# Hymba decoder layer: where split weights are rounded, where sample rows are summed, and when weights are made ready

## The chip, the cores and the metric

The kernel runs on one core of a Trainium2 chip. The core has a matrix engine (TensorE, PE in the profile), three engines for elementwise work (VectorE or DVE, ScalarE or ACT, GpSimd or POOL), and SyncE (SP), whose queue here issues nearly all transfers between the chip's memory (HBM) and the core's SBUF. PE writes its sums into PSUM, which has eight banks of 128 partitions by 512 fp32 numbers. The metric is the device time of one execution in microseconds, as the median of some runs.

## The reference

One layer for a prompt of 2048 rows and for a sample group of 32 rows (8 × 4), with the same weights, all in fp32. `_project` is an RMSNorm and a matrix of 1024 by 2560, `_swiglu` is (silu(h·w_gate) * (h·w_up))·w_down of the normed rows h:

```python
    q, k, v, u, vg = _project(x, norm1_g, w_in)
...
    gate = _spatial_gate(vn, sgu_w, sgu_b).reshape(B, S, D_SGU)
    x = x + jnp.concatenate([att, u * gate], axis=-1) @ w_out
    x = x + _swiglu(x, norm2_g, w_gate, w_up, w_down)
```

Attention has eight heads with three dilated windows each. The hidden width of the FFN is D_FF = 2816, which is 22 units of 128. Results are the rows of both groups after a last RMSNorm, the keys and values, and the normalised rows of the gating unit for the sample.

## The kernel before

**Precision.** PE multiplies a rounded fp32 format. Each fp32 operand is split into a high part (a copy that rounds, made on ACT) and a low part (the rest, a subtraction on DVE or POOL), and each product is three matmuls: high·high, high·low, low·high. So each weight tile costs one ACT copy and one subtraction before PE can use it, in place: the low overwrites the loaded tile.

**Stages.** By the trace: 0–545 us projection, to 850 attention, to 990 the out-projection of the first block, then the FFN of three blocks of rows. Block 0 has 6 tiles of 128 rows (about 990–1455), block 1 has 6 (1560–2030), the last block 4 tiles and the 32 sample rows (2140–2506). Between blocks lies a transition (`next_block`), in which the last down products of the one block are mixed with the out-projection and norms of the next.

**FFN.** Hidden units are taken in pairs. For each unit, seven products (Strassen's scheme over two halves of the columns and of the rows) are made by `one(u, q)`, one per tick of a clock; `later(n, fn)` puts a piece of work n ticks ahead, so the order of all engines is that in which Python emits the pieces. A pair n has seven down products `k = 7n + p`, each at a tick `t_ = 14(n + 1) + SLOT[p]`. The weight of a down product is loaded three products ahead into a ring of three places (two in `hop` tiles, one in `dwx`) and split by `split_dw`, three ticks before its product. ACT makes the high (L1651), and the low (L1652) is on DVE in block 0, on POOL in block 1, and in the last block on DVE for each third product and on POOL for the others. The seven operands of a pair's down products, made from the hidden activations, are also split (L1693, L1689). POOL's main work is the low of the streamed gate and up weights (`op`, L1589), on which it spends 518.8 us. PE's down matmuls are L1667, and DVE adds each result to the rows kept in SBUF (`acc`, L1669). The up products are L1786 to L1788; their sums in PSUM (`ps_m`) are taken out by DVE into `raw` and `zn` (L1798 to L1815).

**Sample rows of the last block.** `hs4` holds the sample's hidden values as 64 columns a unit: high and low side by side, so a product with 64 stationary columns (L1676) gives both parts in the two halves of the partitions. In four of seven down products the sample's rows are multiplied too, into a fresh bank, and DVE adds the bank to the 64-row accumulator once or twice (L1680).

**Transitions.** The output weights are kept as eight pairs of high and low tiles; `half1_place` puts four of them in places that hop tiles leave ("woh", "wol"), `half1_split` splits them (ACT L137, POOL L140) at ticks 14, 16, 18, 20, and `sources` loads the next block's weights for the up products at 16, 18, 20, 22. `split_cat` splits the concatenated attention rows on DVE and POOL in turn. SP's queue holds these loads, the stores of finished rows (`out_yp`) and the loads of the next rows (`acc`) in one order.

**Weight sums.** Strassen's scheme needs sums of down weights. `down_rows` loads them, `down_sums` adds on POOL (tile `tw`, L629), `down_keep` stores them; a plan places them at steps of the projection, pair n from step 124 + 9n. A step is about 2.3 us.

Of the kernel before, what the change touches and what calls it, by code (L numbers as in the profile page):

```python
# [10 lines left out]
F32 = mybir.dt.float32  # L11
# [8 lines left out]
P = 128  # L20
# [44 lines left out]
def hymba_step(ctx: ExitStack, tc: tile.TileContext, A: dict, O: dict):  # L65
# [1269 lines left out]
    def load_acc(B, i):  # L1335
# [4 lines left out]
        else:  # L1340
            dve.memset(x[SR:2 * SR], 0.0)
# [307 lines left out]
    def split_dw(B, k):  # L1649
        hi, lo_ = B.dw[k]  # L1650
        act.activation(hi, lo_.bitcast(F32), AF.Copy)  # L1651
        (dve if B.b0 == 0 or B.last and k % 3 == 0 else pool).tensor_sub(lo_, lo_.bitcast(F32), hi.bitcast(F32))  # L1652

    def down_product(B, k):
# [15 lines left out]
        if B.last and p in (0, 4, 5, 6):  # L1670
            if p < 6:
                B.chain["s"] = ps_m(3)
            ps = B.chain["s"][0:2 * SR]
            hs_ = hs4[:, n % 2 * 2 + (p in (4, 6))]
            for y, r_ in enumerate((dh, dl)):
                pe.matmul(ps, hs_, r_, start=(p < 6 and y == 0), stop=(y == 1), skip_group_check=True)  # L1676
            x = B.acc[B.nt]
            for half in ((0, 1), (0,), (), (1,))[(0, 4, 5, 6).index(p)]:
                cs = slice(half * 512, (half + 1) * 512)
                dve.tensor_add(x[0:2 * SR, cs], x[0:2 * SR, cs], ps)  # L1680
# [59 lines left out]
    def h_last(B, u, part):  # L1740
# [19 lines left out]
        else:  # L1760
# [4 lines left out]
            lows_of(B, 5, u["s1"], 0, n)  # L1765
            lows_of(B, 6, u["s4"], 0, n)
# [62 lines left out]
    def hidden(B, u, zz, c):  # L1829
# [9 lines left out]
        if B.last:  # L1839
            hs_ = hs4[:, f // 2 % 2 * 2 + f % 2]  # L1840
            hi, lo_ = (hs_[:, v * SR:(v + 1) * SR].rearrange("p (z j o c) -> p z j o c", z=2, o=2, j=B.nt // 2)[:, zz] for v in range(2))
# [3 lines left out]
            else:  # L1845
                dve.tensor_sub(lo_, h[:, :, :, 64:], hi.bitcast(F32))

    def plain_down(B, i, half, z, ps, start, stop):

        nr = P if B.rows[i] == P else 2 * SR  # L1850
        dh, dl = B.dw["plain", z, half]
        if nr == P:
            hh, hl = (x[:, i // 2 * P:(i // 2 + 1) * P] for x in B.hop[(0, 2, 4, 3)[2 * z + i % 2]])
            pairs = ((hh, dh), (hh, dl), (hl, dh))
        else:
            hs_ = hs4[:, (NF // 2 - 1) % 2 * 2 + z]
# [560 lines left out]
```

## Time and profile before

| | us |
|---|---|
| median of three runs | 2540.61 (2535.99 to 2541.87) |
| profiled execution | 2534.4 |
| its span, first to last instruction | 2532.6 |
| PE busy | 2410.7 (95%) |
| DVE, POOL, ACT busy | 1705.0, 1457.5, 1236.6 |
| lows of down weights, `hop`, on POOL, DVE | 92.4 (71), 87.0 (72) |
| mean granted clock of PE | 0.984 |

The profiled execution is faster than the median of the timed runs; a sum made from its rows is made against its own time. An engine's busy share is a mean over stages; the waits are read by stage. In a timeline row the number in brackets is how long the engine stood idle before the instruction, and behind the arrow is what released it. L1652 is a line of the kernel before; lines of the changed kernel are a few to twenty higher behind the first edits.

### The profile page before, as it was taken

Reading aid. Unit: us, or ns where it says so; the run is one execution under the profiler, and the core shown is the slowest. Engines: PE = TensorE matmul, PEld = TensorE weight load, DVE = VectorE, ACT = ScalarE, POOL = GpSimd, SP = SyncE. Lnnn points to the kernel's source line nnn. Section 1 sums busy time; section 2 is a strip of 40 time slices with the busy share of each in tenths; the row PEclk is TensorE's granted clock in tenths of the full one; section 3 lists DMA queues with packets and bytes.
Section 4 is the critical chain, followed back from the end, with each engine's and each line's share of the span. In section 5 each row is a group of like instructions: output and inputs, shape, how many; then the busy total and the mean of one; then the engine's idle time right before and its main releaser. Section 6 shows DMA issues by size and latency. Waiting matters only on the chain.

```text
span 2532.6 us, 40744 instructions
## 1 busy us (share of the span) xinstructions
PE 2410.7 (95%) x13764; PEld 2075.1 (82%) x13764; DVE 1705.0 (67%) x3289; ACT 1236.6 (49%) x2773; POOL 1457.5 (58%) x1165
## 2 busy tenths in 40 slices
PE   9998999999999999999999999999999988999997
PEld 7876776657888678899898978999999967888886
DVE  4558673215777644777777786777777776888887
ACT  6324343226676656555566446433334345545444
POOL 2216573214777637676776734666665643767775
PEclk9999999999999999999999999999999998999999
DMA  9874877895555465777776653655555544766673
GB/s 293 272 233 145 275 240 243 268 301 195 195 187 170 118 205 165 225 223 240 237 217 216 201 170 113 198 167 182 172 181 173 161 127 143 236 221 224 213 229 118
DMA packets 331476, 512.38 MB, mean 202 GB/s; under 512 B 33063, under 2 KB 165336, under 8 KB 326148
## 3 DMA queue, kind: packets, MB, share of 16 engines
q1 hardware_dynamic: 324420, 497.72, 61.9%
q10 hardware_dynamic: 6848, 12.06, 1.7%
q8 instruction: 109, 1.79, 0.3%
q14 instruction: 99, 0.81, 0.1%
HBM read 410.42 MB, written 178.03 MB: 232 GB/s over the span
## 4 chain that ended last, share of the span: by engine, by line
PE 54%; DVE 14%; DMA 9%; ACT 8%; issue 7%; POOL 7%; SPq 1%; ACTq 0%; DVEq 0%; POOLq 0%
PE ps_o L1667 7%; PE ps_m L1786 7%; PE ps_m L1788 6%; PE ps_m L1787 6%; PE ps_m L1667 2%; PE ps_s L891 2%; PE ps_o L946 2%; PE ps_s L320 2%; DVE hop L1689 2%; PE ps_s L321 2%; ACT fr L1557 2%; PE ps_s L322 2%; ACT op L1585 2%; DVE acc L1669 2%; POOL op L1589 2%
## 5 line engine op out<-in xcount | busy, mean ns | idle before, releaser
L1589 POOL TENSOR_TENSOR op<-fr,op 128x512 fp32r<-128x512 f32 x385 | 518.8, 1362 | 194.2 <-ACT op L1585 147.0
L1786 PE MATMUL ps_m<-xh,op 128*128 128x384 f32 (+3 forms) x1904 | 608.5, 320 | 17.3 <-DVE raw L1807 11.1
L1788 PE MATMUL ps_m<-xh,op 128*128 128x384 f32 (+3 forms) x1904 | 606.1, 318 | 0.0
L1787 PE MATMUL ps_m<-xl,op 128*128 128x384 f32 (+3 forms) x1904 | 605.3, 318 | 0.1
L1786 PEld LDWEIGHTS ps_m<-xh,op 128*128 128x128 f32 x1904 | 360.7, 189 | 34.6 <-issue 15.4
L1787 PEld LDWEIGHTS ps_m<-xl,op 128*128 128x128 f32 x1904 | 360.7, 189 | 9.3 <-DVE xl L1502 0.4
L1788 PEld LDWEIGHTS ps_m<-xh,op 128*128 128x128 f32 x1904 | 360.4, 189 | 0.0
L1667 PE MATMUL ps_o<-hop 128*128 128x512 f32 x1142 | 325.0, 396 | 18.0 <-DVE acc L1669 17.1
L1669 DVE TENSOR_TENSOR acc<-acc,ps_o 128x512 f32<-128x512 f32 x448 | 290.2, 679 | 17.5 <-PE ps_o L1667 14.5
L1667 PEld LDWEIGHTS ps_o<-hop 128*128 128x128 f32 x1142 | 209.5, 188 | 59.6 <-ACT ps_t L1826 13.9
L1585 ACT ACTIVATE op<-fr 128x512 fp32r<-128x512 f32 x396 | 238.5, 619 | 0.0
L1826 ACT ACTIVATE ps_t<-zn 128x384 f32<-128x384 f32 (+1 forms) x126 | 58.3, 463 | 341.2 <-DVE zn L1809 185.1
L320 PE MATMUL ps_s<-wh,xh 128*128 128x512 f32 x480 | 199.9, 416 | 7.4 <-ACT xh L137 5.9
L321 PE MATMUL ps_s<-wl,xh 128*128 128x512 f32 x480 | 191.4, 399 | 2.0 <-DVE wl L228 2.0
L322 PE MATMUL ps_s<-wh,xl 128*128 128x512 f32 x480 | 191.3, 398 | 0.0
L1652 POOL TENSOR_TENSOR hop<-hop 128x512 fp32r<-128x512 f32 x71 | 92.4, 1302 | 106.1 <-ACT hop L1651 80.7
L1652 DVE TENSOR_TENSOR hop<-hop 128x512 fp32r<-128x512 f32 x72 | 87.0, 1208 | 88.2 <-ACT hop L1651 88.1
L538 POOL TENSOR_TENSOR pr<-kv,qb 96x512 f32<-96x512 f32 x32 | 46.0, 1439 | 168.4 <-DMA kv<-in_cache_k_dram 83.1
L320 PEld LDWEIGHTS ps_s<-wh,xh 128*128 128x128 f32 x480 | 92.6, 193 | 51.1 <-issue 23.9
L1589 POOL TENSOR_TENSOR op<-pair,op 128x512 fp32r<-128x512 f32 x63 | 82.3, 1307 | 75.9 <-ACT op L1585 72.2
L629 POOL TENSOR_TENSOR tw<-tw 128x512 f32<-128x512 f32 x44 | 60.3, 1370 | 113.3 <-DMA tw<-in_w_down_dram 86.8
L1667 PE MATMUL ps_m<-hop 128*128 128x512 f32 x384 | 119.4, 392 | 0.0
(532 smaller groups left out, 5350.7 us busy)
## 6 DMA issues: line engine op xcount, KB each, us to landing
fr<-ab_d SPq DMA_DIRECT2D x308, 256.0 KB
hop<-dd_d SPq DMA_DIRECT2D x143, 256.0 KB
out_ks_dram<-in_cache_k_dram SPq DMA_DIRECT2D x56, 512.0 KB
out_vs_dram<-in_cache_v_dram SPq DMA_DIRECT2D x56, 512.0 KB
ab_d<-fr SPq DMA_DIRECT2D x88, 256.0 KB
dwx<-dd_d SPq DMA_DIRECT2D x71, 256.0 KB
qk_d<-pair SPq DMA_DIRECT2D x64, 256.0 KB
ab_d<-pair SPq DMA_DIRECT2D x63, 256.0 KB
```

Source lines behind the costliest of these rows:

```text
L320: pe.matmul(o[j], xh[:, k, :], wh, start=(k == 0), stop=False)
L321: pe.matmul(o[j], xh[:, k, :], wl, start=False, stop=False)
L322: pe.matmul(o[j], xl[:, k, :], wh, start=False, stop=(k == KD - 1))
L629: pool.tensor_sub(x, y, z)
L1585: act.activation(ops[f, j][0], ab[f][j], AF.Copy)
L1589: (pool if f or j in POOL_LOW else dve).tensor_sub(lo_, ab[f][j], hi.bitcast(F32))
L1652: (dve if B.b0 == 0 or B.last and k % 3 == 0 else pool).tensor_sub(lo_, lo_.bitcast(F32), hi.bitcast(F32))
L1667: pe.matmul(ps, l_, r_, start=(new and y == 0), stop=(y == 2), skip_group_check=True)
L1669: dve.tensor_add(x[:, cs], x[:, cs], ps)
L1786: pe.matmul(out, wh[:, ks], xh[:, :, k], start=(k == 0), stop=False)
L1787: pe.matmul(out, wh[:, ks], xl[:, :, k], start=False, stop=False)
L1788: pe.matmul(out, wl[:, ks], xh[:, :, k], start=False, stop=(k == 3))
```

## The change

Four parts.

1. *Sample rows.* `hs4` goes. Each unit has a place of 192 columns at the end of a big tile, with zeros, 64 columns of data, and zeros or a copy of the data (`rows_at`). A window of 128 of them is the stationary operand, so the data falls into the partitions 0–63 or 64–127 or both: the half of the output columns that a product belongs to is chosen by the window, and all sample products of the block sum up in one bank of PSUM. DVE's adds per pair go; at the end two adds and three copies take the bank out (`last_rows`).
2. *Lows of down weights.* `split_dw` becomes `dw_high`, at three ticks before the product as now, and `dw_low`, at two. In the last block all lows are on POOL; block 0 keeps its own on DVE, but for the last pair.
3. *Transitions.* Output weights take their places in the order wide, wide, ob, ob, and are split at ticks 8, 10, 13, 14; their sources come at 10, 12, 15, 16; `split_cat` is on POOL throughout; the lows of operands 5 and 6 of the last pair move to POOL; the splits of the last seven down weights stand further back.
4. *Weight sums.* Pair n starts at step 118 + 7n, and its parts follow one another two steps closer.

```diff
-        s0 = 124 + 9 * n
+        s0 = 118 + 7 * n
...
-            at(s0 + 9 + part, "out", down_sums, n, part)
-        at(s0 + 13, "store", down_keep, n, 0, 1)
-        at(s0 + 14, "store", down_keep, n, 3, 2)
+            at(s0 + 7 + part, "out", down_sums, n, part)
+        at(s0 + 11, "store", down_keep, n, 0, 1)
+        at(s0 + 12, "store", down_keep, n, 3, 2)
...
-            half1[s // 2] = wide_pair("woh") if s % 4 == 0 else ob_pair("wol")
+            half1[s // 2] = wide_pair("woh") if s < 4 else ob_pair("wol")
...
-    def split_dw(B, k):
+    def dw_high(B, k):
         hi, lo_ = B.dw[k]
         act.activation(hi, lo_.bitcast(F32), AF.Copy)
-        (dve if B.b0 == 0 or B.last and k % 3 == 0 else pool).tensor_sub(lo_, lo_.bitcast(F32), hi.bitcast(F32))
+
+    def dw_low(B, k):
+        hi, lo_ = B.dw[k]
+        (pool if B.b0 or k >= 7 * (NF // 2 - 1) else dve).tensor_sub(lo_, lo_.bitcast(F32), hi.bitcast(F32))
...
         if B.last and p in (0, 4, 5, 6):
-            if p < 6:
-                B.chain["s"] = ps_m(3)
-            ps = B.chain["s"][0:2 * SR]
-            hs_ = hs4[:, n % 2 * 2 + (p in (4, 6))]
-            for y, r_ in enumerate((dh, dl)):
-                pe.matmul(ps, hs_, r_, start=(p < 6 and y == 0), stop=(y == 1), skip_group_check=True)
-            x = B.acc[B.nt]
-            for half in ((0, 1), (0,), (), (1,))[(0, 4, 5, 6).index(p)]:
-                cs = slice(half * 512, (half + 1) * 512)
-                dve.tensor_add(x[0:2 * SR, cs], x[0:2 * SR, cs], ps)
+            v = (64, 64, 0, 0)[(0, 4, 5, 6).index(p)]
+            sample_product(B, 2 * n + (p in (4, 6)), v, dh, dl, k == 0)
+
+    def rows_at(f):
+
+        i = (2 + f % 2 if f // 2 % 2 else f % 2) if f + 2 < NF else 4 + f % 2
+        return pool_["X"][0][:, 7616 + 192 * i:7808 + 192 * i]
...
+    def sample_product(B, f, v, dh, dl, start=False, stop=False):
+
+        if start:
+            B.chain["s"] = ps_m(3)
+        l_ = rows_at(f)[:, v:v + P]
+        for y, r_ in enumerate((dh, dl)):
+            pe.matmul(B.chain["s"], l_, r_, start=start and y == 0, stop=y == 1, skip_group_check=True)
...
-            lows_of(B, 5, u["s1"], 0, n)
-            lows_of(B, 6, u["s4"], 0, n)
+            lows_of(B, 5, u["s1"], 0, n, None, pool)
+            lows_of(B, 6, u["s4"], 0, n, None, pool)
...
-                later((0, 1, 5, 8, 10, 12)[j], split_cat, B, i, dve if j % 2 else pool)
+                later((0, 1, 5, 8, 10, 12)[j], split_cat, B, i, pool)
...
-            later(14 + 2 * y, half1_split, B, 2 * y, 2 * y + 1)
-            later(16 + 2 * y, sources, B, 0, *((2 * y, 2 * y + 1) if y < 3 else (6,)))
+            later((8, 10, 13, 14)[y], half1_split, B, 2 * y, 2 * y + 1)
+            later((10, 12, 15, 16)[y], sources, B, 0, *((2 * y, 2 * y + 1) if y < 3 else (6,)))
...
-        split_dw(prev, K + 1)
         h_last(prev, prev.u, 0)
         downs(K)
         h_last(prev, prev.u, 1)
+        split_dw(prev, K + 1)
+        opens(0)
         split_dw(prev, K + 2)
-        opens(0)
         h_last(prev, prev.u, 2)
         split_dw(prev, K + 3)
+        opens(1)
         split_dw(prev, K + 4)
-        opens(1)
+        downs(K + 1, K + 2, K + 3)
         split_dw(prev, K + 5)
-        downs(K + 1, K + 2, K + 3)
...
                     if x == t_ - 3:
-                        split_dw(B, k)
+                        dw_high(B, k)
+                    if x == t_ - 2:
+                        dw_low(B, k)
```

The order on three engines, before and after. On DVE in a pair of block 0, around the adds into `raw` (L1806, L1807 before; L1820, L1821 in the change). Before:

```order
L1652 TENSOR_TENSOR dwx<-dwx,hop 128x512
L1689 TENSOR_TENSOR hop<-ps_t_10730,hop 128x3x64
...
L1800 TENSOR_TENSOR zn<-zn,ps_m_10955 128x384
L1669 TENSOR_TENSOR acc_9295<-acc_9295,ps_o_10978 128x512
L1669 TENSOR_TENSOR acc_9549<-acc_9549,ps_o_10983 128x512
L1669 TENSOR_TENSOR acc_9643<-acc_9643,ps_m_10988 128x512
L1803 TENSOR_TENSOR zn<-raw,ps_m_10996 128x384
L1652 TENSOR_TENSOR hop<-hop 128x512
L1806 TENSOR_TENSOR raw<-raw,ps_m_11025 128x384
L1807 TENSOR_TENSOR raw<-raw,ps_m_10996 128x384
```

and in the change:

```order
L1814 TENSOR_TENSOR zn<-zn,ps_m_10954 128x384
L1675 TENSOR_TENSOR acc_9295<-acc_9295,ps_o_10977 128x512
L1675 TENSOR_TENSOR acc_9549<-acc_9549,ps_o_10982 128x512
L1675 TENSOR_TENSOR acc_9643<-acc_9643,ps_m_10987 128x512
L1654 TENSOR_TENSOR dwx<-dwx,hop 128x512
L1817 TENSOR_TENSOR zn<-raw,ps_m_10996 128x384
L1820 TENSOR_TENSOR raw<-raw,ps_m_11024 128x384
L1821 TENSOR_TENSOR raw<-raw,ps_m_10996 128x384
L1675 TENSOR_TENSOR acc_9295<-acc_9295,ps_o_10977 128x512
L1675 TENSOR_TENSOR acc_9549<-acc_9549,ps_o_10982 128x512
L1675 TENSOR_TENSOR acc_9643<-acc_9643,ps_m_10987 128x512
L1654 TENSOR_TENSOR hop<-hop 128x512
```

Each low (L1652, now L1654) has moved from ahead of a product's adds to right behind them. On POOL in the last block, where `op` is a streamed weight and `hop` and `dwx` the lows of down weights, before:

```order
L1652 TENSOR_TENSOR hop<-hop 128x512
L1589 TENSOR_TENSOR op<-fr,op 128x512 x2
L1652 TENSOR_TENSOR dwx<-dwx,hop 128x512
L1589 TENSOR_TENSOR op<-fr,op 128x512 x4
L1652 TENSOR_TENSOR hop<-hop 128x512
```

and in the change:

```order
L1654 TENSOR_TENSOR hop<-hop 128x512
L1588 TENSOR_TENSOR op<-fr,op 128x512 x2
L1654 TENSOR_TENSOR hop<-hop 128x512
L1588 TENSOR_TENSOR op<-fr,op 128x512 x2
L1654 TENSOR_TENSOR dwx<-dwx,hop 128x512
```

The third that was on DVE now divides the four `op` lows that stood together. On ACT in the second transition, where "woh" and "wol" are output weights and L1891 (now L1907) sums the squares of finished rows, before:

```order
L1651 ACTIVATE xh_9285<-xl_9286 128x512
L1891 ACTIVATE pair,h_9272<-acc_15602 128x1024
L137 ACTIVATE woh<-fr 128x512 x2
L1891 ACTIVATE pair,h_9272<-acc_15633 128x1024
L1435 ACT_TABLE_LOAD
L1435 ACTIVATE h_9272<-h_9272 128x1
L1891 ACTIVATE pair,h_9272<-acc_15493 128x1024
L137 ACTIVATE wol<-fr 128x512 x2
```

and in the change:

```order
L137 ACTIVATE woh<-fr 128x512 x2
L1650 ACTIVATE xh_9285<-xl_9286 128x512 x2
L137 ACTIVATE woh<-fr 128x512 x2
L137 ACTIVATE wol<-fr 128x512 x2
L1907 ACTIVATE pair,h_9272<-acc_15602 128x1024
L137 ACTIVATE wol<-fr 128x512 x2
L1907 ACTIVATE pair,h_9272<-acc_15633 128x1024
L1434 ACT_TABLE_LOAD
```

The splits of the output weights stand ahead of the first sum of squares or right behind it, instead of between the sums. On SP's queue there, two loads of `fr<-ab_d` that stood between stores of finished rows have moved ahead of the first of these stores.

More of the change, by code (lines that the diff above doesn't have):

```diff
@@ L1340, in load_acc @@
         else:
-            dve.memset(x[SR:2 * SR], 0.0)
             sync.dma_start(x[0:SR], A["x_sample"])
@@ L1839, in hidden @@
         if B.last:
-            hs_ = hs4[:, f // 2 % 2 * 2 + f % 2]
-            hi, lo_ = (hs_[:, v * SR:(v + 1) * SR].rearrange("p (z j o c) -> p z j o c", z=2, o=2, j=B.nt // 2)[:, zz] for v in range(2))
+            hs_ = rows_at(f)
+            hi, lo_ = (hs_[:, 64 + v * SR:64 + (v + 1) * SR].rearrange("p (z j o c) -> p z j o c", z=2, o=2, j=B.nt // 2)[:, zz] for v in range(2))
             act.activation(hi, h[:, :, :, 64:], AF.Copy)
@@ L1846, in hidden, with down_sample @@
                 dve.tensor_sub(lo_, h[:, :, :, 64:], hi.bitcast(F32))
+            if f % 2 == 0 and f + 2 < NF and zz == 0:
+                later(2, lambda: act.activation(hs_[:, 128:192], hs_[:, 64:128].bitcast(F32), AF.Copy))
     def plain_down(B, i, half, z, ps, start, stop):
-        nr = P if B.rows[i] == P else 2 * SR
         dh, dl = B.dw["plain", z, half]
[L1852 to L1856, printed above, removed]
-            pairs = ((hs_, dh), (hs_, dl))
-        for y, (l_, r_) in enumerate(pairs):
-            pe.matmul(ps[0:nr], l_, r_, start=start and y == 0, stop=stop and y == len(pairs) - 1)
+        hh, hl = (x[:, i // 2 * P:(i // 2 + 1) * P] for x in B.hop[(0, 2, 4, 3)[2 * z + i % 2]])
+        pairs = ((hh, dh), (hh, dl), (hl, dh))
+        for y, (l_, r_) in enumerate(pairs):
+            pe.matmul(ps, l_, r_, start=start and y == 0, stop=stop and y == len(pairs) - 1)
+    def down_sample(B):
+        tick()
+        for z in range(2):
+            for half in range(2):
+                sample_product(B, NF - 2 + z, 0 if half else 64, *B.dw["plain", z, half])
     def down_unit(B, i):
         tick()
-        nr = P if B.rows[i] == P else 2 * SR
         for half in range(2):
@@ L1868, in down_unit @@
                 plain_down(B, i, half, z, ps, z == 0, z == 1)
-            dve.tensor_add(B.acc[i][0:nr, cs], B.acc[i][0:nr, cs], ps[0:nr])
+            dve.tensor_add(B.acc[i][:, cs], B.acc[i][:, cs], ps)
     def first_downs(B, i0, i1):
@@ L1949, in last_rows @@
         act.activation(r[:, 0:2], a[:, 2:4], AF.Sqrt)
-        down_unit(B, s)
+        down_sample(B)
         newton(r[:, 0:2], a[:, 2:4])
-        y = square_tile()
-        act.activation(y[0:SR], x[s][SR:2 * SR], AF.Copy)
+        ps, y, w_ = B.chain["s"], square_tile(), square_tile()
+        for z in range(2):
+            cs = slice(z * 512, (z + 1) * 512)
+            act.activation(y[0:SR, cs], ps[64 * z + SR:64 * z + 2 * SR], AF.Copy)
+            if z:
+                act.activation(w_[0:SR, cs], ps[64:64 + SR], AF.Copy)
+            dve.tensor_add(x[s][0:SR, cs], x[s][0:SR, cs], w_[0:SR, cs] if z else ps[0:SR])
         scaled_rows(0, r[:, 0:1])
@@ L2220, in hymba_step @@
         if B.last:
-            hs4 = consts.tile([P, 4, 2 * SR], F32R, name="hs4", tag="cats")
+            sample_rows_free(B)
         nb = None if B.last else blocks[bi + 1]
@@ L2288, in one @@
                     if x == t_ - 3:
-                        split_dw(B, k)
+                        dw_high(B, k)
+                    if x == t_ - 2:
+                        dw_low(B, k)
                     if x == t_:
```

3 lines of the change are left out of this document (added).

## The prediction

> **What bounds the kernel now.** I read the page first, then the clock, then the busy time of each engine by stage, then what TensorE (PE) waited for in each stage.
>
> ```profile
> span 2532.6 us, 40744 instructions
> PE 2410.7 (95%) x13764; PEld 2075.1 (82%) x13764; DVE 1705.0 (67%) x3289; ACT 1236.6 (49%) x2773; POOL 1457.5 (58%) x1165
> ```
>
> PE is busy for 95% of the span. PE's instructions are the same in number and order before and after, so the change can win only the 2532.6 − 2410.7 = 122 us in which PE stands, and what a slow clock costs. The next view is busy time and clock in three stretches: FFN of block 0, of block 1, of the last block (columns: PE, PEld, DVE, ACT, POOL busy, granted clock, DMA share, GB/s).
>
> ```profile
> 1050.00:1450.00 400.00, 390.08 (x2035) 361.24 (x2034) 308.12 (x513) 228.09 (x577) 287.35 (x220) 1.00 0.71 222
> 1600.00:2000.00 400.00, 400.00 (x2109) 375.02 (x2108) 301.18 (x492) 158.17 (x330) 252.47 (x193) 1.00 0.56 175
> 2140.00:2500.00 360.00, 345.93 (x2275) 315.26 (x2274) 298.36 (x584) 175.44 (x417) 256.86 (x193) 1.00 0.68 220
> ```
>
> Block 1 stands for nothing: there the moved lows can only lose. Block 0 stands for 9.9 us in 400, the last block for 14.1 in 360. The waits name the releasers: first 1000–1460, then 2135–2533.
>
> ```profile
> PE ps_m L1786 <- DVE raw L1807: 11.1, 9, 1.3
> ...
> PE ps_o L1667 <- DVE acc L1669: 13.4, 15, 1.8
> ```
>
> Both FFN losses are VectorE (DVE) adds that come late, and each is caused by what stands ahead of the add in DVE's queue. The rest of PE's idle time that the change touches is in the two transitions.
>
> **Block 0: the low moves behind the next adds.** One pair of units (45.55 us) of ten, on DVE, ACT and PE:
>
> ```profile
> 1196.37 1.36 DVE L1652 TENSOR_TENSOR dwx<-dwx,hop 128x512 fp32r<-128x512 f32 x1 [1.39 <-ACT hop L1651]
> 1199.58 1.27 DVE L1669 TENSOR_TENSOR acc<-acc,ps_o 128x512 f32<-128x512 f32 x2
> 1204.16 0.69 DVE L1652 TENSOR_TENSOR hop<-hop 128x512 fp32r<-128x512 f32 x1 [2.24 <-ACT hop L1651]
> ...
> 1201.17 2.44 ACT L1557 ACTIVATE fr<-fr,g2c 128x128 f32<-128x128 f32 x8
> 1203.51 0.61 ACT L1651 ACTIVATE hop<-hop 128x512 fp32r<-128x512 f32 x1
> ...
> 1195.38 0.85 PE L1667 MATMUL ps_m<-hop 128*128 128x512 f32 x3
> 1200.71 0.39 PE L1667 MATMUL ps_o<-dwx,hop 128*128 128x512 f32 x1
> 1206.05 0.41 PE L1786 MATMUL ps_m<-xh,op 128*128 128x384 f32 x1 [1.24 <-DVE raw L1807]
> ```
>
> ACT makes the high at 1203.51 behind eight small ops (2.44 us). DVE's low waits 2.24 us for it, and the two adds into "raw" queue behind that low, so PE waits 1.24 us for a free bank. In the change this low stands three L1669 adds further back, so the "raw" adds no longer queue behind it. Gain: up to 1.24 per pair, in all the 11.1 us of the nine waits.
>
> What is late next: the dwx low ahead of it, now at 1196.37, also moves behind the L1669 adds. These are now two at 1199.58 and a third of the same kind, and end at 1199.58 + 3 × 0.64 = 1201.5. PE had finished their product at 1195.38 + 0.85 = 1196.2, so only DVE's queue holds them, and with the low gone from ahead they end up to 1.36 earlier, at 1200.1. The low then ends between 1200.8 (if it takes 0.69) and 1201.5 (1.36), and PE reads it at 1200.71: a new wait of 0.1 to 0.8 per pair. Chosen, the middle: 10 × (1.24 − 0.45) = **−8**. Bounds: −11 (no new wait), and +9 if the adds don't move up at all and the low is long (1201.5 + 1.36 − 1200.7 = 2.1 per pair), which PE's early end speaks against.
>
> The two lows of this fence, of one shape, took 1.36 and 0.69 us. The Trainium skill ("SBUF — State Buffer", section "Who interferes with whom") says that a DVE instruction with two SBUF inputs and a GpSimd instruction that reads SBUF lock each other out for a whole instruction; the trace fits, since POOL worked beside the first. By that rule a dwx low in block 0 takes the long value, the new wait is 0.8 each, and this term is −4 instead of −8.
>
> **The last block: fewer instructions on DVE, more on POOL.** Groups of 2160–2480, one of the waits, and POOL ahead of a product:
>
> ```profile
> L1652 DVE TENSOR_TENSOR hop<-hop 128x512 fp32r<-128x512 f32 x22 | 27.7, 1257 | 24.0 <-ACT hop L1651 23.9
> L1680 DVE TENSOR_TENSOR acc<-acc,ps_m 64x512 f32<-64x512 f32 x36 | 23.5, 671 | 0.0
> L1652 POOL TENSOR_TENSOR hop<-hop 128x512 fp32r<-128x512 f32 x22 | 28.9, 1313 | 27.4 <-ACT hop L1651 22.2 <-PE ps_o L1667 5.1
> L1676 PE MATMUL ps_m<-hop,hs 128*64 128x512 f32 x62 | 20.1, 390 | 0.0
> L1667 PE MATMUL ps_o<-hop 128*128 128x512 f32 x342 | 97.2, 396 | 11.4 <-DVE acc L1669 11.2
> ...
> 2375.70 0.93 PE L1667 MATMUL ps_o<-hop 128*128 128x512 f32 x3 [1.82 <-DVE acc L1669]
> ...
> 2376.07 1.27 DVE L1680 TENSOR_TENSOR acc<-acc,ps_m 64x512 f32<-64x512 f32 x2
> ...
> 2342.91 2.55 POOL L1589 TENSOR_TENSOR op<-fr,op 128x512 fp32r<-128x512 f32 x2
> 2346.22 1.30 POOL L1652 TENSOR_TENSOR dwx<-dwx,hop 128x512 fp32r<-128x512 f32 x1 [0.75 <-PE ps_o L1667]
> ...
> 2349.49 0.40 PE L1667 MATMUL ps_o<-dwx,hop 128*128 128x512 f32 x1
> ```
>
> DVE loses 27.7 us of lows and 23.5 of sample adds: 51.2 of the 298.4 us it worked in 2140–2500. The waits fall where DVE's adds trail; most are under 1.3, one low or two sample adds long. So most of 13.4 goes. The sample products get a stationary of 128 instead of 64 rows; 390 against 396 ns says that this costs about 62 × 6 ns = 0.4 us. The ten extra ACT copies stand on an engine with 185 idle us. POOL gains 22 lows of 1.313, 28.9 us, and goes from 257 to 286 of 360. That leaves 74 us idle, but a product needs its low at a moment. At 2346.22 the low ends at 2347.52, and PE reads it at 2349.49: 1.97 us to spare. In the change it starts later by one unit, behind two operand lows (2.55 us) at the worst, which makes it 0.6 late; behind one (1.28), it has 0.7 to spare. Chosen: five of 63 products late by 0.6, 3 us, and DVE's waits down to 0.4: −13.4 + 3 + 0.4 = **−10**. Bounds: −13 and +4 (28 products late by 0.6, 17 − 13).
>
> **Block 1** changes only the moment of the low, on POOL: 0 (0 to +2), hidden as long as POOL's idle 147 us (400 − 252.5) lie ahead of the products.
>
> **Transitions.** In the second one PE waits for splits of output weights:
>
> ```profile
> 2080.68 0.45 PE L1419 MATMUL ps_o<-woh,cats 128*64 128x512 f32 x1 [1.39 <-POOL woh L140]
> 2086.39 0.69 PE L1418 MATMUL ps_o<-wol,cats 128*64 128x512 f32 x1 [3.79 <-ACT wol L137]
> 2088.74 0.69 PE L1419 MATMUL ps_o<-wol,cats 128*64 128x512 f32 x1 [1.66 <-POOL wol L140]
> 2104.29 1.05 PE L1479 MATMUL ps_m<-ident,xns 32*128 32x32 f32 x8 [5.85 <-ACT xns L1466]
> ...
> 2066.44 1.06 ACT L1891 ACTIVATE pair<-acc 128x1024 f32<-128x1024 f32 x1 [18.00 <-DVE acc L1669]
> ...
> 2080.65 10.06 SPq L1544 DMA_DIRECT2D fr<-ab_d  x4
> 2091.28 0.38 SPq L1339 DMA_DIRECT2D acc<-in_x_prompt_dram  x1
> ...
> 2097.43 0.69 DVE L1424 TENSOR_TENSOR acc<-acc,ps_m 128x512 f32<-128x512 f32 x1 [4.28 <-DMA acc<-in_x_prompt_dram]
> ```
>
> ACT stands idle for 18 us ahead of 2066.44, and the splits queue behind it. In the change they come first, so the first three waits (6.8 us, with smaller ones 8.4) go. But PE then only comes earlier to the wait for "xns", and that chain hangs on a row load: issued at 2091.28, behind four loads that stood 10.06 us in SP's queue, added on DVE at 2097.43, with PE's start at 2104.29, 13.0 us after the issue. Two of those loads now stand ahead of the first store, and the two that are left still wait for operand lows behind DVE adds of units that PE now ends earlier. Half of the queue's stand gone (5 us), less a place that comes free a little later, I take 3.9 us: the load goes out at 2087.4, an estimate, and PE restarts 13.0 later, at 2100.4: **−4**. PE stands from 2104.29 − 5.85 − 8.4 = 2090.0 on, so this pause grows to 10.4. Bounds: 0 (the load gates as now) and −8.4 (the chain keeps up). In the first block's out-projection the same places are split, and PE waits for none of them now: 0.
>
> The granted clock is 0.57 in 2080–2090 after such pauses:
>
> ```profile
> 2080.00:2090.00 10.00, 3.17 (x6) 0.84 (x6) 7.98 (x16) 3.91 (x9) 5.44 (x4) 0.57 0.37 110
> ```
>
> The Trainium skill ("TensorE: Matmul & The Clock Gate", "What's actually happening") says that an idle window of about 3.4 us halves the clock until as long a busy one has passed. By it the change has one cold start where there are two now, worth an estimated 1.7 us more; the sum leaves it out.
>
> In the first transition:
>
> ```profile
> 1461.15 1.63 PE L1667 MATMUL ps_o<-hop 128*128 128x512 f32 x6 [1.01 <-DVE acc L1669]
> 1469.67 0.50 PE L1414 MATMUL ps_m<-op,xh 128*128 128x512 f32 x1 [0.84 <-POOL op L140]
> 1479.63 0.47 PE L1667 MATMUL ps_o<-xh,hop 128*128 128x512 f32 x1 [1.73 <-DVE acc L1669]
> 1494.07 0.47 PE L1667 MATMUL ps_o<-xh,hop 128*128 128x512 f32 x1 [0.57 <-DVE acc L1669]
> ```
>
> They are 4.15 us, and DVE's splits that held up its adds go to POOL: **−4**; bounds −6 (two more small waits of this kind) and +2 (POOL late by two lows, 2 × 1.3, less one of the four).
>
> **Weight sums** come earlier, into a stretch in which the DMA engines are full, and end ahead of the loads of cached values that PE waits for later:
>
> ```profile
> 300.00:320.00 20.00, 20.00 (x85) 16.34 (x85) 14.02 (x19) 4.65 (x6) 19.12 (x11) 0.92 0.96 281
> PE ps_t L599 <- DMA pr<-in_cache_v_dram: 6.2, 4, 3.4
> ```
>
> More loads at a share of 0.96 delay weights that PE needs; fewer at the end may save the late three of the four waits, 6.2 − 3.4 = 2.8. Chosen **+1**; bounds −3 and +6 (the 6.2 us of such waits a second time); PE's full 20.00 in this window says that weights have some lead. The tail's ACT copies and the one DVE memset: 0 (−1.5 to +1), since the memset stands in the pause before "xns".
>
> **Sum:** −8 − 10 + 0 − 4 − 4 + 1 = −25. The profiled execution took 2534.4 us (span 2532.6), 6.2 less than the median 2540.6; from its own time that is 2509.4, and against the median **2516**.
>
> **The rivals.**
>
> 1. *The row load gates all of the second transition, and the sums crowd the loads.* 0 instead of −4, and +6 instead of +1: 2516 + 4 + 5 = 2525. For it: the 10.06 us that SP stands, and the share 0.96. Against it: two loads of the four do move, and PE was busy for all of that window.
> 2. *DVE's waits only change place.* Each wait was a queue one instruction too long; if ACT's late highs are the true limit (23.9 of 24.0 idle us ahead of DVE's lows are for ACT), lows that now come later hold the products by as much as the adds were held: block 0 and the last FFN at 0, leaving −7: 2534. The change would not do what it says. Against it: 51.2 us of work leave DVE for good.
> 3. *POOL becomes the bound of the last FFN (slower).* All 63 lows are on POOL, which takes its queue in order. If the product's low regularly stands behind two operand lows, it comes 0.6 late (above) each time: 63 × 0.6 − 13 = +25 instead of −10, 2516 + 35 = 2551. It turns the sign once it outweighs the other 15 us, from (15 + 13)/63 = 0.44 us per product. For it: 1.97 to spare against 2.55. Against it: 74 idle us in the stage, and PE's pace per pair leaves POOL to catch up.
> 4. *All at the good end:* −11 − 13 − 8.4 − 6 − 3 = −41, 2499.
>
> **Chances.** Forecast (2506 to 2524) 0.50; rival 1 0.14; rival 2 0.15; rival 3 0.10; rival 4 0.06; something unseen on either side 0.05. A measurement here tells no change from 0.2%, 5 us: 2535.5 to 2545.7. Faster: 0.50 + 0.14 + 0.06 + 0.09 of rival 2 + 0.01 of the unseen = 0.80; same: 0.06 of rival 2, 0.02 of rival 3 and 0.02 of the unseen = 0.10; slower: 0.08 of rival 3 and 0.02 = 0.10. The range takes in the forecast, rivals 1 and 2 and a little on the fast side: **2500 to 2537**.
>
> **What would show it.** Block 0: no wait "L1786 for raw", and DVE's dwx low ending near PE's read of it. Last block: DVE busy near 247 and POOL near 286 of 360 us, waits for "acc" under 1 us in all, and few waits of down products for a POOL low; many of them would be rival 3. Second transition: no waits for "woh" or "wol", one pause of about 10 us before "xns", the row load near 2087. First: the four waits gone. Projection: no new waits for weights in 280–360. I am wrong in the main if PE's idle time in the last FFN stays above 8 us, or if waits for split operands (hop, dwx) take the place of those for adds.

## The result: 1.6% faster, just beyond the range

The changed kernel took 2497.11 us (median of four runs, 2494.55 to 2500.75), the kernel before 2538.3 beside it: a ratio of 0.9844, 95% interval 0.9813 to 0.9875, some 40 us. The prediction was 2516 (25 us less), range 2500 to 2537. The sign was right, and the gain was some 1.6 times the forecast.

The page of the changed kernel, profiled in an execution of 2499.13 us:

```profile
span 2497.3 us, 40725 instructions
PE 2400.0 (96%) x13764; PEld 2081.7 (83%) x13764; DVE 1638.8 (66%) x3209; ACT 1236.7 (50%) x2785; POOL 1502.9 (60%) x1205
```

The three FFN stretches, shifted to about the same work (columns as before: PE, PEld, DVE, ACT, POOL, clock, DMA share, GB/s):

```profile
1034.00:1430.00 396.00, 396.00 (x2086) 371.06 (x2085) 320.85 (x525) 236.23 (x600) 297.62 (x227) 1.00 0.74 232
1589.00:1980.00 391.00, 391.00 (x2061) 366.45 (x2060) 282.23 (x478) 152.29 (x319) 247.07 (x189) 1.00 0.56 175
2125.00:2465.00 340.00, 338.85 (x2280) 317.81 (x2280) 258.68 (x523) 174.71 (x427) 285.45 (x219) 1.00 0.71 231
```

PE's waits in 1000–1460, then in 2135–2533 (us in total, times, longest):

```profile
PE ps_o L1673 <- DVE hop L1654: 3.0, 2, 2.0
PE ps_m L1800 <- DVE raw L1829: 1.4, 1, 1.4
```

```profile
PE ps_o L1870 <- DVE acc L1885: 3.1, 1, 3.1
PE ps_o L1673 <- DVE acc L1675: 1.2, 1, 1.2
PE ps_o L1870 <- DVE acc L1675: 0.8, 1, 0.8
```

PE now stands for nothing in block 0's stretch and for 1.15 us in the last one, where it stood for 9.9 and 14.1 before. The nine waits for `raw` and fourteen of fifteen for `acc` are gone, and no down product of the last block waits for a POOL low. New are two waits for DVE's lows in the first pair of block 0, and a longer one in the tail (L1870, 3.1 us).

Since PE's 13764 matmuls stand in one order in both kernels, each can be set beside its counterpart, and the time from one mark to the next compared. That gives the change by stage, in us of the profiled executions (stages by the times of the kernel before):

| stage | forecast | measured |
|---|---|---|
| projection, 250–545 | +1 | +11.3 |
| attention and first out-projection, 545–990 | 0 | −1.9 |
| block 0, 990–1455 | −8 | −14.8 |
| first transition, 1455–1560 | −4 | −5.5 |
| block 1, 1560–2030 | 0 | +1.5 |
| second transition, 2030–2140 | −4 | −5.7 |
| last FFN, 2140–2506 | −10 | −21.1 |
| tail | 0 | +3.0 |

With −0.3 ahead of 250 and −1.8 behind the last matmul this makes the 35.3 us by which the two spans differ. (By the medians it is some 40: the profiled execution of the kernel before was one of its faster ones, that of the changed kernel one of its slower ones.) The last FFN gave more than the printed waits on which its bound of −13 stood, block 0 more than its bound of −11, and the projection lost more than its bound of +6. All three had to be explained.

### The profile page after: what moved, and what is told of

Read it like the earlier page. It is cut to its first block, busy times and chain, and to the rows that moved or that the text cites. A ratio compares the mean times of both kernels' runs of the same rounds, so it can differ in the third digit from the quotient of the medians.

```text
span 2497.3 us, 40725 instructions
## 1 busy us (share of the span) xinstructions
PE 2400.0 (96%) x13764; PEld 2081.7 (83%) x13764; DVE 1638.8 (66%) x3209; ACT 1236.7 (50%) x2785; POOL 1502.9 (60%) x1205
## 3 DMA queue, kind: packets, MB, share of 16 engines
q10 hardware_dynamic: 6848, 12.06, 1.9%
## 4 chain that ended last, share of the span: by engine, by line
PE 70%; DVE 4%; POOL 2%; ACT 2%; issue 1%; DMA 1%; SPq 0%; DVEq 0%; ACTq 0%; POOLq 0%
PE ps_o L1673 12%; PE ps_m L1800 11%; PE ps_m L1802 11%; PE ps_m L1801 11%; PE ps_m L1673 4%; PE ps_s L891 3%; PE ps_o L946 2%; PE ps_t L918 1%; PE ps_s L320 1%; PE ps_s L970 1%; PE ps_s L322 1%; PE ps_o L1412 1%; PE ps_s L321 1%; PE ps_o L1413 1%; PE ps_o L1414 1%
## 5 line engine op out<-in xcount | busy, mean ns | idle before, releaser
L1588 POOL TENSOR_TENSOR op<-fr,op 128x512 fp32r<-128x512 f32 x385 | 510.1, 1335 | 344.1 <-ACT op L1584 196.6
L1675 DVE TENSOR_TENSOR acc<-acc,ps_o 128x512 f32<-128x512 f32 x448 | 295.6, 682 | 40.2 <-PE ps_o L1673 33.4
L1654 POOL TENSOR_TENSOR hop<-hop 128x512 fp32r<-128x512 f32 x96 | 131.7, 1373 | 0.0
L322 PEld LDWEIGHTS ps_s<-wh,xl 128*128 128x128 f32 x480 | 92.5, 193 | 21.2 <-POOL xl L140 0.4
L1556 ACT ACTIVATE fr<-fr,g2c 128x128 f32<-128x128 f32 x352 | 108.2, 387 | 0.0
```

The costliest lines, as they stand in the source:

```text
L322: pe.matmul(o[j], xl[:, k, :], wh, start=False, stop=(k == KD - 1))
L1556: act.activation(w_[:, k * P:(k + 1) * P], w_[:, k * P:(k + 1) * P], AF.Copy, scale=g2c[:, kk:kk + 1])
L1588: (pool if f or j in POOL_LOW else dve).tensor_sub(lo_, ab[f][j], hi.bitcast(F32))
L1654: (pool if B.b0 or k >= 7 * (NF // 2 - 1) else dve).tensor_sub(lo_, lo_.bitcast(F32), hi.bitcast(F32))
L1675: dve.tensor_add(x[:, cs], x[:, cs], ps)
```

## Experiments

All ratios are to the kernel before, on the same chip, with 95% intervals. Numbers by stage come from the same comparison of matmuls.

### Each part alone

Each of these is the kernel before with one part of the diff. The sums:

```diff
-        s0 = 124 + 9 * n
+        s0 = 118 + 7 * n
...
-            at(s0 + 9 + part, "out", down_sums, n, part)
+            at(s0 + 7 + part, "out", down_sums, n, part)
```

> The kernel before with the weight sums of the change alone. Comparing the two profiles matmul by matmul, the changed kernel falls 11 us behind between 250 and 400 us, beside waits for S_s (5.1 and 3.3 us) that the kernel before doesn't have. Theory 1: the earlier sums fill POOL's queue ahead of the sample attention's products and cost about 8 to 11 us: time 0.3 to 0.45% above the kernel before. Rival: the 11 us are the luck of one execution (DMA order) and the sums cost nothing or win 2.8 us from the cached-value waits: 0.0 to -0.1%.

Measured: 1.0028 (1.0017 to 1.0038), 7 us slower. Between 250 and 420 the kernel falls 9.6 us behind; by 990 it has won back 4.9, though kernels with the sums as before come out between 3.5 us shorter and 0.5 us longer from 420 to 990 too. So the sums do cost, and the change would have been faster without them.

The transitions:

```diff
-            half1[s // 2] = wide_pair("woh") if s % 4 == 0 else ob_pair("wol")
+            half1[s // 2] = wide_pair("woh") if s < 4 else ob_pair("wol")
...
-            later(14 + 2 * y, half1_split, B, 2 * y, 2 * y + 1)
+            later((8, 10, 13, 14)[y], half1_split, B, 2 * y, 2 * y + 1)
```

> The kernel before with the edits to the transitions alone (places, ticks, split_cat, order of splits). Theory 1: the parts add up, so it shows what the two profiles show there: first transition -5.5 us, second -5.7 us, -11 us in all (-0.45%), and the wait for xns grows from 5.8 to about 14.8 us. Rival: the first transition's gain came from the later low or from the block before it, then only the second's -5 (-0.2%).

Measured: 0.9961 (0.9948 to 0.9974). First transition −5.7, second −3.6. The waits for the output weights are gone, and the wait for xns takes most of what they gave; in that kernel, between 2015 and 2140:

```profile
PE ps_m L1479 <- ACT xns L1466: 14.9, 1, 14.9
PE ps_t L1479 <- ACT pair L1532: 4.9, 1, 4.9
PE ps_m L1419 <- POOL op L140: 3.2, 2, 2.7
```

The single bank for the sample rows:

```diff
-            for half in ((0, 1), (0,), (), (1,))[(0, 4, 5, 6).index(p)]:
-                cs = slice(half * 512, (half + 1) * 512)
-                dve.tensor_add(x[0:2 * SR, cs], x[0:2 * SR, cs], ps)
+            v = (64, 64, 0, 0)[(0, 4, 5, 6).index(p)]
+            sample_product(B, 2 * n + (p in (4, 6)), v, dh, dl, k == 0)
```

> The kernel before with the sample rows' single bank alone. DVE loses 23.5 us of 64-row adds in 2160-2480 but keeps its third of the lows. Theory 1 (every us of DVE work ahead of a late add counts): the last FFN gains about 23.5/51.2 of its 21 us, -10 us (-0.4%), less up to 3 us more in the tail. Rival (the lows alone make the adds late): 0 to -3 us.

Measured: 0.9946 (0.9932 to 0.996), the last FFN −13.6 us, the tail +1.6.

The lows:

```diff
-        (dve if B.b0 == 0 or B.last and k % 3 == 0 else pool).tensor_sub(lo_, lo_.bitcast(F32), hi.bitcast(F32))
+        (pool if B.b0 or k >= 7 * (NF // 2 - 1) else dve).tensor_sub(lo_, lo_.bitcast(F32), hi.bitcast(F32))
...
                     if x == t_ - 3:
-                        split_dw(B, k)
+                        dw_high(B, k)
+                    if x == t_ - 2:
+                        dw_low(B, k)
```

> The kernel before with the lows one unit later and on POOL in the last block, and nothing else. Theory 1: block 0 shows the -14 us of the full change, and the last FFN -11 to -17 us: -25 to -30 us (-1.0 to -1.2%). Rival: block 0 -8 as forecast and the last FFN needs both parts to gain, under -15 us in all (-0.6%).

Measured: 0.9834 (0.9818 to 0.985), as much as the whole change: block 0 −14.7, the first transition −4.9, the last FFN −21.9, block 1 +1.5. So both theories sized it too small; the last FFN needs no bank. The four parts alone add up to −1.7 − 0.5 − 0.4 + 0.3 = −2.3%, against −1.6% together: the bank and the lows win the same waits, and so do the transitions and the lows at 1455–1560.

### Later, or on another engine?

Two pieces of that part, each alone, against the kernel before. The low one unit later, with its engine as before:

```diff
                     if x == t_ - 3:
-                        split_dw(B, k)
+                        dw_high(B, k)
+                    if x == t_ - 2:
+                        dw_low(B, k)
```

And the low on POOL in the last block, at its old moment:

```diff
-        (dve if B.b0 == 0 or B.last and k % 3 == 0 else pool).tensor_sub(lo_, lo_.bitcast(F32), hi.bitcast(F32))
+        (pool if B.last else dve if B.b0 == 0 else pool).tensor_sub(lo_, lo_.bitcast(F32), hi.bitcast(F32))
```

A third piece of the part, the lows of block 0's last pair on POOL, was not run by itself.

> The kernel before with each low one unit later, on the engines as before (DVE still has a third in the last block). Theory 1: what counts is the place in the queue, behind the adds: block 0 -14.7 as with the full change, and in the last FFN most of the 21.9. Rival: in the last FFN it is the 27.7 us of DVE work that counts; then block 0 -14.7, last FFN 0 to -7, and the rest comes from the engine.

> The kernel before with all lows of the last block on POOL, three units ahead as before. Theory 1 (place in DVE's queue): a low that isn't in DVE's queue can't hold an add, so the last FFN gains 8 to 22 us, block 0 nothing. Rival 3 of the prediction (POOL bound): with all 63 lows in order on POOL, products wait for them, at 0.6 us each +38 us; less than that if POOL has room.

Measured: later alone 0.9882 (0.9868 to 0.9895), block 0 −14.8, last FFN −12.9. POOL alone 0.9949 (0.9936 to 0.9961), block 0 +0.2, last FFN −11.0. What is left of the down products' waits in the last FFN with later alone:

```profile
PE ps_o L1674 <- DVE acc L1676: 4.4, 6, 1.1
PE ps_o L1674 <- DVE hop L1655: 1.9, 4, 0.5
```

and with POOL alone:

```profile
PE ps_o L1674 <- DVE acc L1676: 9.1, 9, 1.5
```

So each of the three (later, POOL, the bank) shortens the same queue ahead of the same adds by an instruction or two and wins 11.0 to 13.6 us; later and POOL together win 21.9, and the bank on top adds nothing (21.1). Block 0 is the work of the later place alone: no kernel without it moved the block by over 0.3 us. In the first transition later alone wins only 1.3 us and POOL in the last block nothing, where the whole part won 4.9; what is left of its edit, the lows of block 0's last pair on POOL, is the likely source of the other 3.6.

### How much room POOL had

The prediction's rival 3 was that POOL becomes the bound once a low is late. Here POOL makes, ahead of each low of the last block in the changed kernel, a subtraction whose result nobody reads, 256 or 512 columns wide (W):

```diff
         hi, lo_ = B.dw[k]
+        if B.last:
+            pool.tensor_sub(pool_["X"][0][:, 9216:9216 + W], lo_[:, 0:W].bitcast(F32), hi[:, 0:W].bitcast(F32))
```

> The changed kernel, with a subtraction of 128x256 whose result nobody reads ahead of each low of the last block on POOL. POOL was busy for 285.5 of 340 us in the last FFN; 62 products leave 0.88 us of POOL's idle time to each. Rival 3 (lows late as soon as POOL's queue is one step longer): about 0.6 us for each of 63 products, +38 us. Theory (only the sum of POOL's work counts as long as lows are a few us ahead): about 0.7 us more each still fits, 0 to +8 us.

> As the last one, with 128x512, 1.34 us for each low. 62 x 1.34 = 83 us against 54.5 idle: POOL must become the bound by at least 83 - 54.5 = 28 us, by rival 3 in full (each product late by all of 1.34) +83 us. Theory: +28 to +45 us in the last FFN, waits of PE for the lows hop and dwx, nothing elsewhere.

Measured: 0.9861 (0.9845 to 0.9877) and 1.0015 (1.0004 to 1.0025). The last FFN gets 5.6 us longer than in the changed kernel with the half, 43.2 with the full one. The stretch and PE's waits for these lows with 256 columns:

```profile
2125.00:2465.00 340.00, 336.97 (x2246) 312.82 (x2245) 256.63 (x519) 173.81 (x423) 330.73 (x283) 1.00 0.71 230
...
PE ps_o L1675 <- POOL hop L1656: 2.2, 7, 0.7
PE ps_o L1675 <- POOL dwx L1656: 1.2, 4, 0.5
```

and with 512:

```profile
2125.00:2465.00 340.00, 316.90 (x2031) 281.44 (x2029) 243.41 (x468) 157.22 (x385) 331.45 (x254) 1.00 0.65 210
...
PE ps_o L1675 <- POOL hop L1656: 16.9, 32, 1.2
PE ps_o L1675 <- POOL dwx L1656: 7.7, 15, 0.8
```

With 256 columns POOL is at 330.7 of 340 us, 97%, and PE has lost 3.4 us to it in waits; with 512 POOL can do no more and PE waits on 47 lows. So rival 3's mechanism exists, but it begins where POOL's work fills the stage. That the low comes one queue step later is not enough. The full one is the point where all the change's gain is spent.

### What the sums' 10 us are

Reading the two profiles I had taken the new waits for S_s to mean that POOL's additions hold up the sample's attention products. The kernel with the early sums, without these additions (the stored sums of down weights are then the plain weights):

```diff
         for x, y, z in (((b11, b12, b11), (b12, b22, b12)), ((b22, b22, b11),), ((b21, b21, b22),))[part]:
-            pool.tensor_sub(x, y, z)
+            pass
```

> The kernel before with the earlier weight sums, but POOL's additions of the sums left out (down weights are stored as they were loaded), all loads and stores kept. What it leaves out is 60 us of POOL work in the projection. With the additions, 250 to 420 was 9.6 us longer. Theory (POOL's queue holds the sample attention's products): the 9.6 us are gone. Rival (the DMA engines are too full for the weights, as forecast): they stay, +6 to +10 us between 250 and 420.

Measured: 1.0017 (1.0006 to 1.0028); 250 to 420 is still 6.5 us longer than before, against 9.6 with the additions. The stretch with the additions:

```profile
300.00:320.00 20.00, 16.73 (x72) 12.91 (x70) 11.90 (x15) 4.65 (x6) 19.51 (x13) 1.00 0.96 288
320.00:340.00 20.00, 16.12 (x73) 13.11 (x74) 14.81 (x20) 6.88 (x11) 15.80 (x12) 1.00 0.91 302
```

and without:

```profile
300.00:320.00 20.00, 17.80 (x79) 14.41 (x80) 12.47 (x19) 3.97 (x6) 12.72 (x7) 1.00 0.98 302
320.00:340.00 20.00, 17.19 (x71) 13.84 (x70) 10.61 (x18) 9.00 (x14) 5.61 (x4) 0.91 0.96 326
```

POOL falls from 35.3 to 18.3 of 40 us and PE still stands for 5.0 of them, with the DMA share at 0.96 to 0.98. So my theory on POOL fell for some two thirds of the loss (6.5 us in this one trace, 9.6 to 11.2 in the four with the additions): it is the early loads and stores, or their places in SP's queue. PE waits for no weight between 250 and 420 in any of the five kernels with early sums. Its new waits are for tiles of the sample (`S_s`, `zn`), and longer ones for the gating unit's rows (`vnh`, 3.4 to 6.7 us, and 1.7 to 3.8 in the kernels with the sums as before). One, in the kernel without additions, can be followed back (PE, DVE, ACT):

```profile
327.71 0.65 PE L585 MATMUL ps_t<-ident,S_s 128*128 128x128 f32 x3 [2.81 <-DVE S_s L579]
...
325.72 0.75 DVE L228 SCALAR_TENSOR_TENSOR wl<-raw,g1c,wh 128x512 fp32r<-128x512 f32 x1 [2.19 <-ACT wh L222]
...
324.96 0.72 ACT L222 ACTIVATE wh<-raw,g1c 128x512 fp32r<-128x512 f32 x1 [3.00 <-DMA raw<-in_w_in_dram]
```

A weight's load comes late, ACT's high and DVE's low of that weight with it (the kernel before makes that high without a wait, at 322.40), and S_s, which stands behind that low in DVE's queue, reaches PE 2.81 us late. So late weights, the forecast's mechanism, do take part, but through DVE's queue and not by a wait of PE for a weight. Loads, stores and the queue were not told apart, and the other waits were not followed back.

### Versions that beat both

The changed kernel with the lines of the sums as they were:

```diff
-        s0 = 118 + 7 * n
+        s0 = 124 + 9 * n
...
-            at(s0 + 7 + part, "out", down_sums, n, part)
+            at(s0 + 9 + part, "out", down_sums, n, part)
```

> The changed kernel with the weight sums at their old steps. The sums alone cost 0.28% (7 us) and 9.6 us of profile between 250 and 420, 5 of them given back by 990. Theory 1 (parts add up by stage): 5 to 8 us under the changed kernel, ratio to the kernel before 0.982 to 0.980, faster than both. Rival: the cost came only together with the old rest of the kernel: 0.984 as the full change.

Measured: 0.9809 (0.9795 to 0.9822), 2488.53 us; 250 to 420 is at +0.3. Theory 1 held.

The two parts of the diff for the lows and for the transitions together, without bank and sums; against the changed kernel this is, at its heart,

```diff
-            v = (64, 64, 0, 0)[(0, 4, 5, 6).index(p)]
-            sample_product(B, 2 * n + (p in (4, 6)), v, dh, dl, k == 0)
+            for half in ((0, 1), (0,), (), (1,))[(0, 4, 5, 6).index(p)]:
+                cs = slice(half * 512, (half + 1) * 512)
+                dve.tensor_add(x[0:2 * SR, cs], x[0:2 * SR, cs], ps)
...
-        s0 = 118 + 7 * n
+        s0 = 124 + 9 * n
```

> The kernel before with the lows and the transitions, without the single bank and without the sums. The lows alone give 42 us, and the last FFN is at 4 us of lost time with them, so the bank has nothing left to win there and costs 1.6 to 3 us in the tail. Theory 1: -42 and half of the transitions' 10 (the first transition's 5 us are the same ones that the lows win): -46 to -48 us, ratio 0.981 to 0.982. Rival: the bank is needed under the transitions' order, 0.984.

Measured: 0.9812 (0.9798 to 0.9825), 2486.39 us. The last FFN is at −21.9 and the tail at 0. The bank isn't needed beside the lows. In each of the five kernels that have it, the time from the last FFN to the end of the span is 1.1 to 1.2 us longer (1.6 to 3.2 up to the last matmul, less 0.4 to 2.1 behind it).

To this the last version adds two edits:

```diff
-                    if x == t_ - 2:
+                    if x == (t_ - 3 if B.b0 and not B.last else t_ - 2):
                         dw_low(B, k)
...
+            if n != P:
+                rms_b(s1, n)
+                norm2_b(B, i, s1, put_off)
+                return
             later(1, rms_b, s1, n)
```

> Lows and transitions without bank and sums (ratio 0.9812), with block 1's lows at their old moment, and in the second transition the sample's norm following its sum at once, ahead of the add that waits for the row load. Block 1: -1.5 us. Second transition: the wait for xns was 14.8 us and the load and what follows it held DVE from 2080.2 to 2084.5, while the sample's rows were summed at 2077.1. If only DVE's order holds that chain, PE restarts 7 us earlier; if the row load gates PE's next wait (pair, 4.9 us) too, it wins 0 to 3. Expected -2 to -8: ratio 0.978 to 0.9805.

Measured: 0.9786 (0.9771 to 0.9801), 2481.7 us, the fastest of all here, though its interval touches those of the last two. Block 1's lows back at their old moment take its +1.5 to 0.0, so that was the price of the later low there. The sample's norm at once halves the wait for xns, but new small waits come behind it (2015–2130):

```profile
PE ps_m L1483 <- ACT xns L1470: 7.6, 1, 7.6
PE ps_t L1483 <- ACT pair L1536: 4.9, 1, 4.9
PE ps_m L1419 <- POOL op L140: 2.7, 2, 2.2
PE ps_t L1483 <- DVE acc L1424: 1.1, 1, 1.1
PE ps_m L1483 <- DVE xl L140: 0.9, 2, 0.6
```

Set beside the kernel with lows and transitions alone, PE loses 3.0 us ahead (1.4 at the operand's low, 2.2 in the rows, the rest at a low clock behind it), wins 7.2 at xns, and gives 4.0 back at later waits. The stage as a whole stays at −7.4, as without the edit. So xns was held by its place in DVE's queue, behind the add that waits for the row load, but PE's restart is not what bounds the stage. What does is not shown: the first three row loads go out 3.4 to 3.5 us later here (the first at 2068.49 for 2064.96), and the stage's end differs by 0.3.

## Why the prediction was wrong

The step that failed is the pricing of PE's waits in the two largest terms, the last FFN and block 0: place and cause were right, the sizes were not. I took the brackets that the profile prints as the price of a wait, and I charged new waits for late lows that did not come. A third term, the projection, missed the other way. So the sum stands closer to the outcome than its terms do: −18 us of misses in the FFNs and +10 in the projection cancel in part, which is luck.

**The last FFN: −10 against −21.1.** Two things in the term were mis-sized. First, I took a wait to cost what its bracket prints. The two rows around one wait of the kernel before:

```profile
2165.75 0.29 PE L1788 MATMUL ps_m<-xh,op 128*128 128x272 f32 x1
2167.36 0.93 PE L1667 MATMUL ps_o<-hop 128*128 128x512 f32 x3 [1.33 <-DVE acc L1669]
```

From start to start it is 1.61 us. Where PE runs, matmuls of 272 columns start 0.126 us apart (the median there), though each is drawn 0.29 long. So this wait cost close to 1.49, not 1.33: the pipelined tail of the matmul before hides 0.16 of it, and waits shorter than the tail aren't printed at all. In 2140–2506, some 40 matmuls start late by over 0.08 us against the median for their kind, by 20.4 us in all (about 1.5 us of it in a short dip of the pace at 2482); printed for them are 13.6. In the changed kernel 1.7 us of such late starts are left; most of what the stage won beyond that are starts late by less. (The wait of 0.8 at L1859 stands in both kernels, at L1870 in the change, and won nothing.) Second, I charged 3.4 us for waits that remain, 3 of them for lows that come too late on POOL. None did:

```profile
2334.89 1.29 POOL L1654 TENSOR_TENSOR dwx<-dwx,hop 128x512 fp32r<-128x512 f32 x1
2338.47 0.40 PE L1673 MATMUL ps_o<-dwx,hop 128*128 128x512 f32 x1
```

This low ends at 2336.18, 2.3 us ahead of its read. The low of the product that I had priced ends at 2322.46 now, 1.9 us ahead of its read, where 1.97 stood before. I had put two operand lows in front of it at the worst. In the order, each low now stands between pairs of operand lows where four stood together. And POOL had stood idle for 27.4 us ahead of its `hop` lows, mostly for ACT's highs, as the prediction's rows show; now the highs are there when the lows' turn comes (2144–2448):

```profile
L1654 POOL TENSOR_TENSOR hop<-hop 128x512 fp32r<-128x512 f32 x44 | 59.4, 1351 | 0.0
```

The kernels with added POOL work (above) show how much room is left.

**Block 0: −8 against −14.8.** Right that the adds into `raw` would no longer queue behind the low. Wrong on the price again: from a matmul ahead of the wait at 1206.05 to one behind it (1202.09 to 1208.06 before, 1204.88 to 1209.35 in the change) the time is 1.50 us shorter, where the bracket prints 1.24. Ahead of most of these waits some 0.2 more is won at a late start that no view prints. And wrong on what is late next: I charged 0.45 per pair for the dwx low. Its add before, and then the changed kernel (DVE, then PE's read):

```profile
1200.78 0.67 DVE L1669 TENSOR_TENSOR acc<-acc,ps_m 128x512 f32<-128x512 f32 x1
...
1201.01 0.68 DVE L1675 TENSOR_TENSOR acc<-acc,ps_m 128x512 f32<-128x512 f32 x1
1201.61 1.28 DVE L1654 TENSOR_TENSOR dwx<-dwx,hop 128x512 fp32r<-128x512 f32 x1
...
1203.49 0.40 PE L1673 MATMUL ps_o<-dwx,hop 128*128 128x512 f32 x1
```

The low ends at 1202.89, 0.6 ahead of the read. I let the adds move up by the low's 1.36 us and left out the bracket in its own row: DVE had also stood for 1.39 us ahead of that low, for ACT's high, and everything behind it in the queue waited along. A low that is moved takes its wait with it. Before, the third add ended 0.7 us behind PE's first read of that low (1200.71); now it ends 1.8 us ahead of it, 2.5 earlier of the 2.75. The first pair of the block, where waits of 2.6, 0.8 and 0.4 us went and two for DVE's lows came (2.0 and 1.0, with a slow pace behind the first), lost 0.4. Nine waits of 1.5 us and eight starts of 0.2, less that, come to 14.7 of the 14.8. The long value of the low, 1.28 against 0.68 for the next one of that shape, is what the Trainium skill's rule gave ("SBUF — State Buffer", "Who interferes with whom"), and the trace agrees with it here: POOL worked beside the first, from 1201.05 on, and stood beside the second, at 1206.31. It cost nothing, since the low had that much room.

**The projection: +1 against +11.3,** beyond the bound of +6. The forecast had early loads, at a DMA share of 0.96, delay weights that PE needs. Some two thirds of the loss do stay without POOL's additions, but PE waits for no weight there; one of its new waits, for a tile of the sample, stands behind a late weight in DVE's queue (above). The path was wrong and the size far too small. POOL's additions, which the forecast didn't name, are the other third (a split good to some 2 us, by which this stretch varies). I took PE's full 20 us in one window as a sign that weights had lead; that window stands next to the only wait between 280 and 360. Some of it came back later, as hoped: the cached-value waits fell from 6.2 to 2.3, and lie at 1.7 to 2.9 in all five kernels with early sums, at 5.0 to 6.6 in the others.

**The transitions** were nearly right: −5.5 for −4 and −5.7 for −4. The step on xns held: the row load holds it, through DVE's queue. I had it go out 3.9 us earlier, and it went out 6.7 earlier (at 2074.85 for 2091.28, of which 9.7 us were won ahead of the stage); PE restarted 12.2 us behind it, at 2087.05, for the 13.0 assumed. So the restart came 7.5 us earlier and not 3.9; of that the stage kept 5.7, and part of what it gave back went to a longer slow stretch behind the pause. That −4 lies so near is luck in part. The pause grew to 14.8, since PE reached it 16.4 us sooner, and not by the 8.4 us of waits that I had counted. The load in the changed kernel, and DVE's wait for it:

```profile
2065.71 8.57 SPq L1543 DMA_DIRECT2D fr<-ab_d  x2
2074.85 0.38 SPq L1339 DMA_DIRECT2D acc<-in_x_prompt_dram  x1
...
2080.19 0.69 DVE L1423 TENSOR_TENSOR acc<-acc,ps_m 128x512 f32<-128x512 f32 x1 [4.07 <-DMA acc<-in_x_prompt_dram]
```

SP still stands 8.57 us behind two loads where four cost 10.06. The first transition's gain comes from the lows' edit alone as well (−4.9), so two parts claim it: each takes lows off DVE there.

The clock around that pause, in windows of 10 us:

```profile
2065.00:2075.00 10.00, 7.29 (x33) 5.32 (x31) 6.75 (x18) 3.76 (x9) 0.00 (x0) 1.00 0.29 93
2075.00:2085.00 10.00, 0.00 (x0) 0.00 (x0) 5.49 (x11) 2.73 (x7) 1.26 (x1) 0.60 0.62 205
2085.00:2095.00 10.00, 7.95 (x26) 6.41 (x27) 5.49 (x24) 6.23 (x18) 0.00 (x0) 0.54 0.52 189
```

While the clock is low, matmuls of 512 columns start 0.43 us apart instead of 0.23. In the kernel before such starts cost 5.7 us in three places of the stage; now 3.0 in one. That is 2.7 us for an estimate of 1.7 by the rule of the Trainium skill ("TensorE: Matmul & The Clock Gate", "What's actually happening"), which I had left out of the sum. The trace agrees with the rule that the pace halves; the slow stretch lasted some 7 us here (2087.05 to 2094.2), and 4.4 us in the kernel with lows and transitions alone, not the 3.4 that I took from it.

**Block 1 and the tail,** forecast 0 and 0, cost 1.5 and 3.0. The first is the later low on POOL, shown by putting it back; the second comes with the bank: alone it costs 1.6, in the full change 3.0, and the tail's longest wait is 3.1 us (L1870) where it was 1.5 (L1859). DVE's two adds of the sample rows, the second waiting for a copy on ACT, stand ahead of the last tiles' adds there. Counted to the end of the span both cost 1.2: in the full change the last twelve matmuls run at a lower clock behind that wait (4.4 us; behind the same wait they take 3.0 in the kernel with the old sums), and the span's end is no later for it.

**The rivals.** Rival 1's half on the sums came true, with the other half not. Rival 2, that waits only change place, was half true for the transitions and not for the FFNs. Rival 3 was shown to need some 0.7 us more POOL work per product than the change makes. Rival 4, all at the good end, at 2499, was nearest to the outcome, at a chance of 0.06; its bounds of −13 for the last FFN and −11 for block 0 were both passed, because both stood on printed waits.

## What to carry to other kernels

Cost a wait of PE from start to start, less the pitch of the matmuls around it, and not by the bracket: behind short matmuls the bracket leaves out the tail of the one before, and small waits altogether. When an instruction moves back in an in-order queue, its own wait for another engine moves along, so what stood behind it moves up by nearly both. And when several edits shorten one queue ahead of the same add, measure each alone: three here won 11 to 14 us each and 21 together, and one of them, the bank, added nothing to the other two and cost time at another place.

## What was not expected of the hardware

A stage of the FFN repeats to hundredths between kernels: block 0 between 1100 and 1455 came out 12.06 us shorter in each of the eight kernels with the later low, while 250 to 420, where the DMA share reaches 0.96 and more, moved by −2.3 to +1.7 us between kernels that don't differ from the one before there. GpSimd was filled to 97% of the last FFN for a loss of 5.6 us, which is further than I would have trusted an in-order queue that PE depends on 63 times.
